# A hybrid decoder layer on one core: substitution rows padded to 36, attention values as one wide product, other stage offsets

## The chip, the cores and the metric

The kernel runs on one core of one Trainium2 chip. Its time is the device time of one execution in microseconds (us); the runs shown are single executions of the same program. The profile is of one further execution and counts its span from the first instruction to the last.

## The reference

One layer of a decoder trunk, 16 meta tokens and 512 frames of width 1024, all in float32. A half-step SwiGLU comes first, then two token mixers that read the same projection, then a second half-step SwiGLU and a norm.

```
h += 1/2 * SwiGLU_1(rmsnorm(h))
P  = rmsnorm(h) @ w_in            # q|k|v, rwkv r|k|v|w|a|g, two gates
A  = sliding-window attention, 16 query heads, 2 key heads, window 128, meta always visible
R  = RWKV-7: per head S = S*w + (S a) b' + v k',  y = S r     (16 heads of 64)
h += (sigmoid(Ga) * (A @ Wa) + sigmoid(Gr) * (R @ Wr)) @ w_out
h += 1/2 * SwiGLU_2(rmsnorm(h))
```

The attention's last steps are `p = e / (sum(e) + exp(sink - m))` and `o = p @ v`. The recurrence S is computed in chunks of 64 tokens; inside a chunk it needs the inverse of a unit lower triangular 64x64 matrix for each head.

## The kernel before

**Stages in time.** In the first 400 us the first SwiGLU runs: weights come by DMA (`raw`), ScalarE makes a rounded copy (`whi`, line 144), VectorE the remainder (`wlo`, line 145), and each product is three matmuls (lines 155 to 157). From 400 to 1130 us the mixer runs, then the output product and the second SwiGLU.

**The mixer** is written as Python generators that `run` interleaves: `qkv`, `attend`, `gates`, `att_branch`, `reload`, `rwkv_branch`, and for each of eight pairs of heads j the stages `stage_a1` (projections, decays), `stage_p` (products of a chunk, the matrices G.g2 to invert), `stage_i` (the inverses), `stage_b` (the recurrence over nine chunks) and `stage_t` (norm, gate). Each task has a start and a span in units of one pair (`PLAN`, plus `SHIFT` for a pair's stage), and `run` always takes the next step of the task whose due time is smallest. `LATE` adds to the priority number under which a step's instructions are handed to the scheduler, so a negative value puts them earlier. The scheduler then fixes one order of instructions for every engine ahead of the run. TensorE (PE), VectorE (DVE), ScalarE (ACT), GpSimd (POOL) and the DMA queue of SyncE (SP) each take their own list strictly in this order, and an instruction that waits holds all behind it on its engine. SP's list holds the loads of weights as well as the stages' own transfers.

**The inverses, `stage_i`.** `stage_p` leaves 32x32 triangles, nine of the upper and eight of the lower half of the chunks for each of the two heads, 34 in all, and writes them to a DRAM tile `Ls` with one triangle in a row. `stage_i` loads `Ls` three times into the tile LT (line 865, `LT<-Ls`), 34 partitions each, 102 in use, and unit columns into X (line 866). Then 31 steps of substitution follow on VectorE, each a product into `xtmp` (line 870) and a sum into X (line 872). The solutions go to the DRAM tile `Xs` (line 876) and from there, transposed, into `xt` (lines 881 and 882). `assemble` completes the 64x64 inverses with two groups of matmuls (lines 898 and 908) that read LT and `xt`. LT and X have one buffer each, so the loads of pair j+1 wait for the end of `assemble` of pair j.

**The recurrence, `stage_b`.** For each chunk: two matmuls with the state W (line 928), a copy `zy` on ScalarE (929), one matmul with `xt` (936), copies into W on VectorE and ScalarE (937, 938), two matmuls (941), and the new state W on VectorE (945 or 947). Each waits for the one before.

**Attention, `attend`.** For each of eight blocks b of 64 queries and two halves i: scores for four groups of 128 rows (x = key head and pair of heads) by at most 208 keys, exponentials `st` in SBUF with their sums `rsum`; `st` transposed by TensorE to `pT` (keys by 512); then, for each of one or two parts of the keys, the product with the values `vt` (line 600: `pT` of one group stands in the array, 64 columns of `vt` move), a multiplication with 1/sum on VectorE (603), a transpose back (608), a copy (611) and two DMAs into `aD` (613).

Of the kernel before, what the change touches and what calls it, by code (L numbers as in the profile page):

```python
# [17 lines left out]
P = 128  # L18
# [18 lines left out]
RB = {"g1": 2, "g2": 2, "W": 2, "g3": 2}  # L37
COUNTS = []
PAUSE = {"sq": 1, "rn": 1, "el": 1, "inv": 1}
PLAN = {"qkv": (-2.771, 0.729), "stage_a1": (-2.83, 0.789), "stage_p": (-1.171, 0.942), "stage_i": (-2.734, 0.587),  # L40
        "stage_b": (-0.138, 0.693), "stage_t": (1.478, 0.214), "att": (-1.614, 1.044), "gate": (0.091, 0.42),
        "att_branch": (3.86, 1.399), "reload": (6.425, 0.417), "rwkv_branch": (7.903, 0.124)}
# [3 lines left out]
SHIFT = {("stage_t", 5): -0.415, ("stage_i", 7): 0.482, ("stage_b", 2): 0.071, ("stage_a1", 6): -0.027, ("stage_i", 4): -0.133,  # L46
        ("stage_t", 2): -0.095, ("stage_b", 3): 0.119, ("stage_p", 1): 0.042, ("stage_t", 4): 0.123, ("stage_t", 3): -0.157,
        ("stage_t", 0): 0.003, ("stage_i", 6): 0.096, ("stage_p", 2): 0.173, ("stage_i", 3): -0.27, ("stage_i", 2): -0.033,
        ("stage_a1", 3): 0.319, ("stage_p", 6): 0.183, ("stage_a1", 4): 0.07, ("stage_p", 3): -0.095, ("stage_i", 1): 0.055,
        ("stage_t", 6): -0.097, ("stage_p", 7): 0.076, ("stage_b", 0): 0.067, ("stage_i", 5): -0.243, ("stage_b", 6): 0.153,  # L50
        ("stage_p", 4): 0.028, ("stage_b", 4): -0.102, ("stage_a1", 0): 0.006, ("stage_a1", 2): 0.186, ("stage_b", 1): -0.009,
        ("stage_t", 7): -0.124, ("stage_t", 1): -0.07, ("stage_i", 0): 0.174, ("stage_p", 5): -0.03, ("stage_b", 7): -0.047}

FIRST = [(0, 0), (0, 1), (1, 0), (1, 1), (27, 0)]
ATTS = 0.946
GATE = 0.462
LATE = {"gate": 337, "att_branch": 1714, "reload": 1055, "rwkv_branch": 2849, "stage_a1": -79, "stage_t": 196, "stage_p": -207,
        "stage_i": -1108, "qkv": -36, "att": 209, "stage_b": 148}
# [50 lines left out]
def hybrid_layer(ctx: ExitStack, tc: tile.TileContext, a, phases="all"):  # L109
# [243 lines left out]
    def mixer(nm):  # L353
# [183 lines left out]
        def attend():  # L537
# [3 lines left out]
            for b in range(NCH):  # L541
# [18 lines left out]
                for i in range(2):  # L560
# [22 lines left out]
                                             accum_out=rsum[:, kv, k:k + 1])  # L583
                    nc.vector.tensor_add(out=rsum, in0=rsum, in1=sm)
                    nc.vector.reciprocal(out=rsum, in_=rsum)
                    yield
                    pTs = []
                    for q, (k0, k1) in enumerate(parts):
# [4 lines left out]
                        nc.scalar.copy(out=pT[:k1 - k0], in_=pt[:k1 - k0])  # L593
                        pTs.append(pT)
                    yield
                    po = bank("att")[:, :4 * CH].rearrange("t (p d) -> t p d", p=4)
                    for x in range(4):
                        kv = x // 2
                        for q, (k0, k1) in enumerate(parts):
                            nc.tensor.matmul(po[:, x, :], pTs[q][:k1 - k0, P * x:P * x + P], vt[:k1 - k0, q, CH * kv:CH * kv + CH],  # L600
                                             start=(q == 0), stop=(q == len(parts) - 1))
                    on = ap.tile([P, 4, CH], F32, name="ao", bufs=1)
                    nc.vector.tensor_tensor(out=on, in0=po, in1=rsum.rearrange("p g k -> p (g k)").unsqueeze(2).to_broadcast([P, 4, CH]),
                                            op=OP.mult)
                    yield
                    pt = bank("att")
                    for kv in range(2):
                        nc.tensor.transpose(out=pt[:, P * kv:P * kv + P], in_=on[:, 2 * kv:2 * kv + 2, :].rearrange("t p d -> t (p d)"),
                                            identity=ident)
                    ao = ap.tile([P, 2, 2, CH], F32, name="ao", bufs=1)  # L610
                    nc.scalar.copy(out=ao, in_=pt[:, :4 * CH].rearrange("p (g x t) -> p g x t", g=2, t=CH))
                    for kv in range(2):
                        nc.sync.dma_start(out=aD[:, 4 * kv + 2 * i:4 * kv + 2 * i + 2, CH * b:CH * b + CH], in_=ao[:, kv])
                    yield

        def gates():
# [151 lines left out]
        def stage_p(j, G):  # L768
# [35 lines left out]
                    m = m.unsqueeze(1).to_broadcast(list(dst.shape))  # L804
                nc.vector.tensor_mul(out=dst, in0=src, in1=m)

            G.Ls = dsc.tile([34, 32, 32], F32, name="Ls")
            for h, U, Vr in ((0, LO, HI), (1, HI, LO)):
                g1, Z, Y = G.g1[h], U, Vr
                pt = bank("s")  # L810
                nc.tensor.matmul(pt[:, 0:P], KBT[:, 0, :], G.g0[:, h, :], start=True, stop=True)
                masked(G.g2[U, 0, :], pt[U, Z], 0)
                masked(G.g0[Vr, h, Z], pt[Vr, Z], 0)
                for c0 in (1, 5):
                    pt = bank("s")
# [12 lines left out]
            nc.tensor.matmul(pb, C("bones"), rkk, start=True, stop=True)
# [27 lines left out]

        def stage_i(j, G):

            Xs = dsc.tile([34, 33, 32], F32, name="Xs")
            G.LT = sp.tile([P, 32, 32], F32, name="LT", bufs=1)  # L860
            LT = G.LT[:102]
            X = sp.tile([102, 11, 32], F32, name="X", bufs=1)
            tmp = sp.tile([102, 11, 32], F32, name="xtmp", bufs=1)
            for q in range(3):
                nc.sync.dma_start(out=LT[34 * q:34 * q + 34], in_=G.Ls)
            nc.sync.dma_start(out=X, in_=a["xinit"])
            yield
            for c in range(31):
                n, w = c // 3 + 1, 31 - c
                nc.vector.tensor_tensor(out=tmp[:, :n, :w], in0=LT[:, c:c + 1, c + 1:32].to_broadcast([102, n, w]),  # L870
                                        in1=X[:, :n, c:c + 1].to_broadcast([102, n, w]), op=OP.mult)
                nc.vector.tensor_add(out=X[:, :n, c + 1:32], in0=X[:, :n, c + 1:32], in1=tmp[:, :n, :w])
                if c % 8 == 7:
                    yield
            for q in range(3):
                nc.sync.dma_start(out=Xs[:, q:33:3, :], in_=X[34 * q:34 * q + 34])
            G.xt = XT[j % 2]
            nc.gpsimd.memset(G.LT[:, :24, :], 0.0)
            for h in range(2):
                u, m = 64 * h, 17 * h  # L880
                nc.sync.dma_start(out=G.xt[u:u + 32, :, u:u + 32], in_=Xs[m:m + 9, 0:32, :].rearrange("c s t -> s c t"))
                nc.sync.dma_start(out=G.xt[u + 32:u + 64, 1:, u + 32:u + 64],
                                  in_=Xs[m + 9:m + 17, 0:32, :].rearrange("c s t -> s c t"))
# [263 lines left out]
def constants():  # L1147
    c = np.zeros((P, NCON), np.float32)

    def put(n, x):  # L1150
        c[:x.shape[0], CON[n]:CON[n] + x.shape[1]] = x
    put("ident", np.eye(P, dtype=np.float32))
    i = np.arange(P)[:, None] % CH
    jj = np.arange(192)[None, :]
    win = np.where((jj > i) & (jj <= 128 + i), 0.0, 8 * NEG).astype(np.float32)
    z = np.zeros((P, NMETA), np.float32)
    put("am", np.concatenate([win, z], 1))
    b = (np.arange(P)[:, None] // CH == np.arange(P)[None, :] // CH).astype(np.float32)
# [16 lines left out]
def prepare(x, meta_tokens, norm_ffn1, ffn1_w_in, ffn1_w_out, norm_mix, w_in, rwkv_mu, sinks, w0, w2, a0, a2, g2, k_k, k_a,  # L1175
# [53 lines left out]
```

## Time and profile before

| what | value |
|---|---|
| three runs | 1551.87, 1556.44 (median), 1558.58 us |
| the profiled execution | 1557.82 us, its span 1556.1 us |
| mean granted TensorE clock | 0.98 |
| TensorE matmul busy, of the span | 1500.3 us (96%) |
| VectorE busy | 900.1 us (58%) |
| ScalarE busy | 652.9 us (42%) |

Busy times are means over stages that differ: VectorE is light in the two SwiGLUs and heavy in the mixer. A matmul's duration in the profile holds the time through the array, in which the next ones already run, so times between starts are shorter than durations. "Idle before" an instruction is the time in which its engine had nothing running, and the name behind it is what ended last before it began.

### The profile page before, as it was taken

The numbers are of one execution on the slowest core, as the hardware profiler recorded it, in microseconds if no ns is written. First come the engines' busy times: TensorE is split into PE (matmuls) and PEld (weight loads), VectorE is DVE, ScalarE is ACT, GpSimd is POOL, SyncE is SP. The second block draws the span as 40 slices with busy tenths as digits, with TensorE's granted clock in tenths as the row PEclk, the third lists the DMA queues.
The fourth block names the chain that finished last, engine by engine and source line by source line (L and its number), as shares of the span: only waits on it lengthen the run. The fifth ranks groups of instructions, "written<-read, shape, count | busy, mean of one in ns | idle before, by whom it ended". The sixth has DMA issues, their size and how long they took to land. (4 is left out here: it accounts for less than half of the span.)

```text
span 1556.1 us, 25641 instructions
## 1 busy us (share of the span) xinstructions
PE 1500.3 (96%) x9365; PEld 1325.2 (85%) x9365; DVE 900.1 (58%) x2471; ACT 652.9 (42%) x1468; POOL 93.6 (6%) x153
## 2 busy tenths in 40 slices
PE   9999999999999999998999999999999999999997
PEld 9999999999887888887878887677777888888886
DVE  6334334344764886887978888675655444443334
ACT  5333333233442457465664754635343333332231
POOL 0111111000100000000000000000000111110000
PEclk9999999999999999999989999999999999999998
DMA  5333333344243333323332232555633333333332
GB/s 165 89 93 91 89 93 88 110 120 116 78 121 96 112 84 89 81 81 104 99 98 76 82 101 85 153 183 173 221 95 89 95 95 96 97 97 91 95 97 79
DMA packets 137838, 163.23 MB, mean 105 GB/s; under 512 B 56960, under 2 KB 68288, under 8 KB 137712
## 3 DMA queue, kind: packets, MB, share of 16 engines
q1 hardware_dynamic: 137568, 161.54, 35.4%
q8 instruction: 73, 1.20, 0.3%
q14 instruction: 53, 0.43, 0.1%
q10 hardware_dynamic: 144, 0.06, 0.0%
HBM read 140.03 MB, written 21.52 MB: 104 GB/s over the span
## 5 line engine op out<-in xcount | busy, mean ns | idle before, releaser
L144 ACT CAST whi<-raw 128x512 fp32r<-128x512 f32 (+1 forms) x426 | 258.8, 611 | 576.6 <-PE dn L156 446.5
L145 DVE TENSOR_TENSOR wlo<-raw,whi 128x512 fp32r<-128x512 f32 (+1 forms) x426 | 287.9, 679 | 304.1 <-ACT whi L144 300.0
L155 PE MATMUL dn<-uh,whi 128*128 128x264 f32 (+1 forms) x1320 | 426.8, 323 | 1.9 <-DVE tgt L657 0.9
L156 PE MATMUL dn<-ul,whi 128*128 128x264 f32 (+1 forms) x1320 | 427.3, 324 | 0.3 <-DVE ul L203 0.3
L157 PE MATMUL dn<-uh,wlo 128*128 128x264 f32 (+1 forms) x1320 | 425.0, 322 | 0.0
L155 PEld LDWEIGHTS dn<-uh,whi 128*128 128x128 f32 x1320 | 247.8, 188 | 23.9 <-ACT whi L144 3.2
L157 PEld LDWEIGHTS dn<-uh,wlo 128*128 128x128 f32 x1320 | 248.4, 188 | 19.9
L156 PEld LDWEIGHTS dn<-ul,whi 128*128 128x128 f32 x1320 | 248.4, 188 | 19.0 <-DVE ul L203 0.5
L155 PE MATMUL pdn<-uh,whi 128*128 128x264 f32 (+3 forms) x656 | 229.0, 350 | 4.6 <-ACT whi L144 2.5
L157 PE MATMUL pdn<-uh,wlo 128*128 128x264 f32 (+3 forms) x656 | 224.3, 343 | 3.7 <-DVE wlo L145 3.6
L156 PE MATMUL pdn<-ul,whi 128*128 128x264 f32 (+3 forms) x656 | 224.5, 343 | 0.9 <-DVE ul L253 0.8
L155 PEld LDWEIGHTS pdn<-uh,whi 128*128 128x128 f32 x656 | 127.1, 194 | 17.0 <-ACT whi L144 4.2
L157 PEld LDWEIGHTS pdn<-uh,wlo 128*128 128x128 f32 x656 | 127.0, 194 | 11.4 <-DVE wlo L145 5.0
L156 PEld LDWEIGHTS pdn<-ul,whi 128*128 128x128 f32 x656 | 126.7, 193 | 7.7 <-DVE ul L253 1.7
L155 PE MATMUL dn<-mh,whi 128*128 128x264 f32 (+2 forms) x350 | 110.7, 316 | 0.0
L156 PE MATMUL dn<-ml,whi 128*128 128x264 f32 (+2 forms) x350 | 110.6, 316 | 0.0
L157 PE MATMUL dn<-mh,wlo 128*128 128x264 f32 (+2 forms) x350 | 110.5, 316 | 0.0
L285 POOL TENSOR_TENSOR sg<-sg,rstd 128x528 f32<-128x528 f32 (+1 forms) x44 | 58.0, 1319 | 595.8 <-ACT sg L284 428.9
L286 DVE TENSOR_TENSOR m<-sg,dn 128x528 f32<-128x528 f32 (+1 forms) x44 | 30.6, 696 | 70.9 <-PE dn L157 67.6
L155 PEld LDWEIGHTS dn<-mh,whi 128*128 128x128 f32 x350 | 66.1, 189 | 4.4
L156 PEld LDWEIGHTS dn<-ml,whi 128*128 128x128 f32 x350 | 66.1, 189 | 4.3
L157 PEld LDWEIGHTS dn<-mh,wlo 128*128 128x128 f32 x350 | 66.0, 189 | 4.3
(395 smaller groups left out, 2058.2 us busy)
## 6 DMA issues: line engine op xcount, KB each, us to landing
raw<-win SPq DMA_DIRECT2D x104, 256.0 KB
raw<-w1in SPq DMA_DIRECT2D x88, 256.0 KB
raw<-w2in SPq DMA_DIRECT2D x88, 256.0 KB
raw<-w1out SPq DMA_DIRECT2D x40, 256.0 KB
raw<-w2out SPq DMA_DIRECT2D x40, 256.0 KB
gD<-tgt SPq DMA_DIRECT2D x24, 256.0 KB
raw<-wa SPq DMA_DIRECT2D x16, 256.0 KB
tgt<-gD SPq DMA_DIRECT2D x16, 256.0 KB
```

Source lines behind the costliest of these rows:

```text
L144: nc.scalar.copy(out=hi, in_=raw)
L145: (eng or nc.vector).tensor_tensor(out=lo, in0=raw, in1=hi.bitcast(F32), op=OP.subtract)
L155: nc.tensor.matmul(o, hi, xh[k][:, c], start=(k == 0), stop=False)
L156: nc.tensor.matmul(o, hi, xl[k][:, c], start=False, stop=False)
L157: nc.tensor.matmul(o, lo, xh[k][:, c], start=False, stop=last)
L285: nc.gpsimd.tensor_mul(out=sg, in0=sg, in1=nm.rstd[:, :n])
L286: nc.vector.tensor_mul(out=vw(m), in0=vw(sg), in1=vu)
```

## The change

Three things change. The rows of `Ls`, `Xs`, LT, X and `xtmp` become 36 (18 for each head) and 108 instead of 34 and 102: the lower half has a ninth row for the meta chunk, which is written and solved but not read back. The attention multiplies `st` by 1/sum before it is transposed, and takes the product with the values as one matmul for each part of the keys: `vt` (both key heads, 128 columns) stands in the array and all 512 columns of `pT` move. Its result lies with the value channels on partitions, so the transpose back falls away; of each key head's 64 rows only the 256 columns of its own queries are copied out, by two copies, and one DMA writes `aD`. The rows of the packed attention weights (`wa`) are put in the matching order on the host. Third, the tables `PLAN`, `SHIFT` and `LATE` and the spacing `ATTS` get other numbers.

```diff
-PLAN = {..., "stage_i": (-2.734, 0.587), ...
+PLAN = {..., "stage_i": (-1.378, 0.919), ...
...
-LATE = {..., "stage_i": -1108, "qkv": -36, "att": 209, "stage_b": 148}
+LATE = {..., "stage_i": -1815, "qkv": -42, "att": 209, "stage_b": 148}
 # attend
                     nc.vector.reciprocal(out=rsum, in_=rsum)
+                    sv = st.rearrange("p g k s -> p (g k) s")[:, :, :n]
+                    nc.vector.tensor_tensor(out=sv, in0=sv, in1=rsum.rearrange("p g k -> p (g k)").unsqueeze(2).to_broadcast([P, 4, n]),
+                                            op=OP.mult)
                     yield
...
-                    po = bank("att")[:, :4 * CH].rearrange("t (p d) -> t p d", p=4)
-                    for x in range(4):
-                        kv = x // 2
-                        for q, (k0, k1) in enumerate(parts):
-                            nc.tensor.matmul(po[:, x, :], pTs[q][:k1 - k0, P * x:P * x + P], vt[:k1 - k0, q, CH * kv:CH * kv + CH], ...)
-                    on = ap.tile([P, 4, CH], F32, name="ao", bufs=1)
-                    nc.vector.tensor_tensor(out=on, in0=po, in1=rsum...to_broadcast([P, 4, CH]), op=OP.mult)
+                    po = bank("att")
+                    for q, (k0, k1) in enumerate(parts):
+                        nc.tensor.matmul(po, vt[:k1 - k0, q, :], pTs[q][:k1 - k0], start=(q == 0), stop=(q == len(parts) - 1))
                     yield
-                    pt = bank("att")
-                    for kv in range(2):
-                        nc.tensor.transpose(out=pt[:, P * kv:P * kv + P], in_=on[:, 2 * kv:2 * kv + 2, :]..., identity=ident)
-                    ao = ap.tile([P, 2, 2, CH], F32, name="ao", bufs=1)
-                    nc.scalar.copy(out=ao, in_=pt[:, :4 * CH].rearrange("p (g x t) -> p g x t", g=2, t=CH))
-                    for kv in range(2):
-                        nc.sync.dma_start(out=aD[:, 4 * kv + 2 * i:4 * kv + 2 * i + 2, CH * b:CH * b + CH], in_=ao[:, kv])
+                    ao = ap.tile([P, 4, CH], F32, name="ao", bufs=1)
+                    pv = po.rearrange("p (g x t) -> p g x t", g=2, t=CH)
+                    for kv, rows in enumerate((LO, HI)):
+                        nc.scalar.copy(out=ao[rows], in_=pv[rows, kv])
+                    nc.sync.dma_start(out=aD[:, 4 * i:4 * i + 4, CH * b:CH * b + CH], in_=ao)
 # stage_p
-            G.Ls = dsc.tile([34, 32, 32], F32, name="Ls")
+            G.Ls = dsc.tile([36, 32, 32], F32, name="Ls")
...
-                nc.sync.dma_start(out=G.Ls[17 * h + 9:17 * h + 17]..., in_=G.g2[u + 32:u + 64, 1:, 32:64])
+                nc.sync.dma_start(out=G.Ls[18 * h + 9:18 * h + 18]..., in_=G.g2[u + 32:u + 64, :, 32:64])
 # stage_i
-                nc.sync.dma_start(out=LT[34 * q:34 * q + 34], in_=G.Ls)
+                nc.sync.dma_start(out=LT[36 * q:36 * q + 36], in_=G.Ls)
...
-                nc.sync.dma_start(out=Xs[:, q:33:3, :], in_=X[34 * q:34 * q + 34])
+                nc.sync.dma_start(out=Xs[:, q:33:3, :], in_=X[36 * q:36 * q + 36])
```

**Where instructions move.** On VectorE, at the start of the substitution of pair 4 (`xtmp<-LT,X` is its first step, `kbt` are `stage_p`'s products for a later pair, `W` the state of the recurrence that runs at that time). Before:

```order
L937 COPY W<-pn 64x64
L870 TENSOR_TENSOR xtmp<-LT,X 102x31
L584 TENSOR_TENSOR rsum<-rsum,sm 128x4
L792 SCALAR_TENSOR_TENSOR kbt<-tal,tE_9024 64x8x64
L872 TENSOR_TENSOR X<-X,xtmp 102x31
L585 RECIPROCAL rsum<-rsum 128x4
L794 SCALAR_TENSOR_TENSOR kbt<-tal,tE_9024 64x16
L870 TENSOR_TENSOR xtmp<-LT,X 102x30
L792 SCALAR_TENSOR_TENSOR kbt<-tk,tE_9024 64x8x64
L872 TENSOR_TENSOR X<-X,xtmp 102x30
L947 SCALAR_TENSOR_TENSOR W<-py,f,sf 64x64
```

The same place after the change (`st<-st,rsum` is the new multiplication, `wlo<-raw,whi` the remainder of a weight block):

```order
L787 SCALAR_TENSOR_TENSOR kbt<-tal,tE_8959 64x8x64
L789 SCALAR_TENSOR_TENSOR kbt<-tal,tE_8959 64x16
L787 SCALAR_TENSOR_TENSOR kbt<-tk,tE_8959 64x8x64
L584 TENSOR_TENSOR rsum<-rsum,sm 128x4
L789 SCALAR_TENSOR_TENSOR kbt<-tk,tE_8959 64x16
L585 RECIPROCAL rsum<-rsum 128x4
L587 TENSOR_TENSOR st<-st,rsum 128x832
L446 SCALAR_TENSOR_TENSOR tk<-pdn,omm,tm 128x264
L933 COPY W<-pn 64x64
L145 TENSOR_TENSOR wlo<-raw,whi 128x512 x2
L941 TENSOR_SCALAR W<-py,f 64x64 x2
L866 TENSOR_TENSOR xtmp<-LT,X 108x31
```

Before, the products `kbt` and the next state W stood behind the first step of the substitution; now they stand ahead of it.

On SP, from the store of the solutions to the loads of `xt`, for pair 4. Before:

```order
L986 DMA g2w<-g2s 128x256
L624 DMA gD<-tgt 128x512
L876 DMA Xs<-X 374x1x32 x3
L881 DMA xt_4608<-Xs 32x9x32
L882 DMA xt_4608<-Xs 32x8x32
```

And after the change:

```order
L994 DMA rD<-tys 128x512
L872 DMA Xs<-X 396x1x32 x3
L608 DMA aD<-ao 128x4x64
L143 DMA raw<-win 128x512 x2
L877 DMA xt_4608<-Xs 32x9x32
L878 DMA xt_4608<-Xs 32x8x32
```

Two loads of weights and one store of attention now stand between the store of the solutions and the loads of `xt`.

On TensorE, block 1 of the attention (`patt<-con,st` are transposes of `st`, `patt<-vt,pT` the product with the values, `pdn` a projection, `ps` products of `stage_p`). Before:

```order
L591 MATMUL patt<-con,st 16x128 x4
L837 MATMUL ps<-con,kbt 128x128 x4
L157 MATMUL pdn<-uh,wlo 128x512
L600 MATMUL patt<-vt,pT 128x64 x8
L837 MATMUL ps<-con,kbt 128x128 x4
L845 MATMUL ps<-con,tv 16x128
L155 MATMUL pdn<-uh,whi 128x512
L156 MATMUL pdn<-ul,whi 128x512
L608 MATMUL patt<-con,ao 128x128 x2
```

After:

```order
L594 MATMUL patt<-con,st 16x128 x4
L156 MATMUL pdn<-ul,whi 128x512
L157 MATMUL pdn<-uh,wlo 128x512
L155 MATMUL pdn<-uh,whi 128x512
L156 MATMUL pdn<-ul,whi 128x512
L602 MATMUL patt<-pT,vt 128x512 x2
L157 MATMUL pdn<-uh,wlo 128x512
```

Eight narrow products and two transposes have become two wide products.

More of the change, by code (lines that the diff above doesn't have):

```diff
@@ L39 @@
 PAUSE = {"sq": 1, "rn": 1, "el": 1, "inv": 1}
-PLAN = {"qkv": (-2.771, 0.729), "stage_a1": (-2.83, 0.789), "stage_p": (-1.171, 0.942), "stage_i": (-2.734, 0.587),
-        "stage_b": (-0.138, 0.693), "stage_t": (1.478, 0.214), "att": (-1.614, 1.044), "gate": (0.091, 0.42),
-        "att_branch": (3.86, 1.399), "reload": (6.425, 0.417), "rwkv_branch": (7.903, 0.124)}
+PLAN = {"qkv": (-2.725, 0.766), "stage_a1": (-2.739, 0.789), "stage_p": (-1.216, 0.962), "stage_i": (-1.378, 0.919),
+        "stage_b": (0.017, 0.693), "stage_t": (1.509, 0.192), "att": (-1.581, 1.044), "gate": (0.017, 0.425),
+        "att_branch": (3.926, 0.992), "reload": (6.358, 0.258), "rwkv_branch": (7.491, 0.149)}
@@ L43 @@
 STEPS = {"qkv": 30, "stage_a1": 19, "stage_p": 13, "stage_i": 9, "stage_b": 27, "stage_t": 5, "att": 13, "gate": 2, "att_branch": 24, "reload": 7,
          "rwkv_branch": 16}
-SHIFT = {("stage_t", 5): -0.415, ("stage_i", 7): 0.482, ("stage_b", 2): 0.071, ("stage_a1", 6): -0.027, ("stage_i", 4): -0.133,
-        ("stage_t", 2): -0.095, ("stage_b", 3): 0.119, ("stage_p", 1): 0.042, ("stage_t", 4): 0.123, ("stage_t", 3): -0.157,
-        ("stage_t", 0): 0.003, ("stage_i", 6): 0.096, ("stage_p", 2): 0.173, ("stage_i", 3): -0.27, ("stage_i", 2): -0.033,
+SHIFT = {("stage_t", 5): -0.415, ("stage_i", 7): 0.36, ("stage_b", 2): 0.071, ("stage_a1", 6): -0.027, ("stage_i", 4): -0.613,
+        ("stage_t", 2): -0.095, ("stage_b", 3): 0.119, ("stage_p", 1): 0.042, ("stage_t", 4): 0.159, ("stage_t", 3): -0.157,
+        ("stage_t", 0): 0.003, ("stage_i", 6): 0.096, ("stage_p", 2): 0.173, ("stage_i", 3): -0.295, ("stage_i", 2): -0.235,
@@ L54 @@
 FIRST = [(0, 0), (0, 1), (1, 0), (1, 1), (27, 0)]
-ATTS = 0.946
+ATTS = 0.961
 GATE = 0.462
-LATE = {"gate": 337, "att_branch": 1714, "reload": 1055, "rwkv_branch": 2849, "stage_a1": -79, "stage_t": 196, "stage_p": -207,
-        "stage_i": -1108, "qkv": -36, "att": 209, "stage_b": 148}
+LATE = {"gate": 160, "att_branch": 1153, "reload": -297, "rwkv_branch": 3776, "stage_a1": -79, "stage_t": 196, "stage_p": -207,
+        "stage_i": -1815, "qkv": -42, "att": 209, "stage_b": 148}
 S_DECAY = float(np.exp(np.float32(-0.5)))
@@ L823, in stage_p @@
                 u = 64 * h
-                nc.sync.dma_start(out=G.Ls[17 * h:17 * h + 9].rearrange("c s t -> s c t"), in_=G.g2[u:u + 32, :, 0:32])
-                nc.sync.dma_start(out=G.Ls[17 * h + 9:17 * h + 17].rearrange("c s t -> s c t"), in_=G.g2[u + 32:u + 64, 1:, 32:64])
+                nc.sync.dma_start(out=G.Ls[18 * h:18 * h + 9].rearrange("c s t -> s c t"), in_=G.g2[u:u + 32, :, 0:32])
+                nc.sync.dma_start(out=G.Ls[18 * h + 9:18 * h + 18].rearrange("c s t -> s c t"), in_=G.g2[u + 32:u + 64, :, 32:64])
             yield
@@ L857, in stage_i @@
         def stage_i(j, G):
-            Xs = dsc.tile([34, 33, 32], F32, name="Xs")
+            Xs = dsc.tile([36, 33, 32], F32, name="Xs")
             G.LT = sp.tile([P, 32, 32], F32, name="LT", bufs=1)
-            LT = G.LT[:102]
-            X = sp.tile([102, 11, 32], F32, name="X", bufs=1)
-            tmp = sp.tile([102, 11, 32], F32, name="xtmp", bufs=1)
+            LT = G.LT[:108]
+            X = sp.tile([108, 11, 32], F32, name="X", bufs=1)
+            tmp = sp.tile([108, 11, 32], F32, name="xtmp", bufs=1)
             for q in range(3):
-                nc.sync.dma_start(out=LT[34 * q:34 * q + 34], in_=G.Ls)
+                nc.sync.dma_start(out=LT[36 * q:36 * q + 36], in_=G.Ls)
             nc.sync.dma_start(out=X, in_=a["xinit"])
@@ L869, in stage_i @@
                 n, w = c // 3 + 1, 31 - c
-                nc.vector.tensor_tensor(out=tmp[:, :n, :w], in0=LT[:, c:c + 1, c + 1:32].to_broadcast([102, n, w]),
-                                        in1=X[:, :n, c:c + 1].to_broadcast([102, n, w]), op=OP.mult)
+                nc.vector.tensor_tensor(out=tmp[:, :n, :w], in0=LT[:, c:c + 1, c + 1:32].to_broadcast([108, n, w]),
+                                        in1=X[:, :n, c:c + 1].to_broadcast([108, n, w]), op=OP.mult)
                 nc.vector.tensor_add(out=X[:, :n, c + 1:32], in0=X[:, :n, c + 1:32], in1=tmp[:, :n, :w])
@@ L879, in stage_i @@
             for h in range(2):
-                u, m = 64 * h, 17 * h
+                u, m = 64 * h, 18 * h
                 nc.sync.dma_start(out=G.xt[u:u + 32, :, u:u + 32], in_=Xs[m:m + 9, 0:32, :].rearrange("c s t -> s c t"))
                 nc.sync.dma_start(out=G.xt[u + 32:u + 64, 1:, u + 32:u + 64],
-                                  in_=Xs[m + 9:m + 17, 0:32, :].rearrange("c s t -> s c t"))
+                                  in_=Xs[m + 10:m + 18, 0:32, :].rearrange("c s t -> s c t"))
             yield
@@ L1159, in constants @@
     put("bones", b)
-    x = np.zeros((102, 11, 32), np.float32)
+    x = np.zeros((108, 11, 32), np.float32)
     for gcol in range(3):
@@ L1163, in constants @@
             if 3 * ii + gcol < 32:
-                x[34 * gcol:34 * gcol + 34, ii, 3 * ii + gcol] = 1
+                x[36 * gcol:36 * gcol + 36, ii, 3 * ii + gcol] = 1
     return c, x
```

12 lines of the change are left out of this document (3 added, 9 removed).

## The prediction

> **What bounds the kernel now.** I read the page's head first, then the busy times by stage, then who waits in the mixer, and last the seconds around those waits. The runs' 0.5% (7.8 us of the median) is about what a measurement of this kernel can tell from no change.
>
> ```profile
> span 1556.1 us, 25641 instructions
> PE 1500.3 (96%) x9365; PEld 1325.2 (85%) x9365; DVE 900.1 (58%) x2471; ACT 652.9 (42%) x1468; POOL 93.6 (6%) x153
> ```
> ```profile
> core 0: us, PE busy (x) PEld busy (x) DVE busy (x) ACT busy (x) POOL busy (x), PEclk, DMA share, GB/s
> 0.00:400.00 400.00, 397.51 (x3222) 395.17 (x3222) 168.72 (x263) 137.65 (x224) 30.24 (x31) 1.00 0.36 106
> 530.00:1060.00 530.00, 497.35 (x3159) 425.67 (x3157) 416.91 (x1601) 296.61 (x855) 24.36 (x69) 0.96 0.36 104
> 1130.00:1556.00 426.00, 415.16 (x1882) 341.85 (x1880) 180.68 (x308) 134.74 (x219) 28.59 (x22) 0.99 0.32 93
> ```
>
> TensorE bounds the whole, and in the two SwiGLUs (first and last row) it hardly idles at full clock. The change touches only the mixer. There, from 530 to 1060 us, TensorE idles 530 - 497.4 = 32.6 us and its granted clock is 0.96, so some 21 us more of clock are missing. VectorE is busy 417 of 530 us (79%). So what the change can save is work on TensorE, idle time, and half-clock time of this stretch. Who waits there:
>
> ```profile
> L870 DVE TENSOR_TENSOR xtmp<-LT,X x248: 163/220/259, 544.0 to 1037.9; 102x84 f32<-102x84 f32 x12, 102x54 f32<-102x54 f32 x8, 102x90 f32<-102x90 f32 x8, 102x72 f32<-102x72 f32 x8
> ...
>   DMA LT<-Ls: 10.8, 5
>   issue: 3.2, 1
>   DMA vt<-vD: 2.7, 1
> ```
> ```profile
> 796.83 0.19 DVE L870 TENSOR_TENSOR xtmp<-LT,X 102x31 f32<-102x31 f32 x1 [3.17 <-issue]
> ...
> 799.00 0.65 PE L928 MATMUL pn<-W,g1e 128*128 128x64 f32 x2 [2.74 <-DVE W L947]
> ...
> 866.52 0.19 DVE L870 TENSOR_TENSOR xtmp<-LT,X 102x31 f32<-102x31 f32 x1 [2.77 <-DMA LT<-Ls]
> ...
> 868.40 0.69 PE L928 MATMUL pn<-W,g1e 128*128 128x64 f32 x2 [2.07 <-DVE W L947]
> ...
> 938.79 0.19 DVE L870 TENSOR_TENSOR xtmp<-LT,X 102x31 f32<-102x31 f32 x1 [2.62 <-DMA LT<-Ls]
> ...
> 940.91 0.67 PE L941 MATMUL py<-W,g 128*128 128x64 f32 x4 [2.23 <-DVE W L937]
> ```
>
> The first step of the substitution stops VectorE seven times, 10.8 + 3.2 + 2.7 = 16.7 us, in seven of the eight pairs, whatever name the row gives the releaser. Behind it in VectorE's list stands the state W, so TensorE stops each time: in the three pairs shown 2.74 + 2.07 + 2.23 = 7.04 us for 3.17 + 2.77 + 2.62 = 8.56 us, or 0.82 us for each. The transfer is slow:
>
> ```profile
> 927.38 1.01 SPq L865 DMA_DIRECT2D LT<-Ls  x3
> ...
> 1039.20 4.70 SPq L876 DMA_DIRECT2D Xs<-X  x3
> ...
> 1048.04 0.33 SPq L881 DMA_DIRECT2D xt<-Xs  x1
> ...
> 1049.41 0.46 SPq L882 DMA_DIRECT2D xt<-Xs  x1
> ```
> ```profile
> 1050.96 0.46 PE L936 MATMUL pn<-zy,xt 128*128 128x128 f32 x2 [2.79 <-DMA xt<-Xs]
> ```
> ```profile
>   DMA xt<-Xs: 7.9, 5
> ```
>
> LT (three loads of 136 KB) is issued at 927.4 and VectorE goes on at 938.8, 11.4 us later. The store of the solutions is issued at 1039.2, and the reads of it start only at 1048.0, 8.8 us later. The last read, of 32 KB with 32 rows outermost, releases TensorE 1.55 us after its start. All loads of `xt` together cost TensorE 7.9 us in five waits (the last row, from line 936). And after a stop the clock is halved:
>
> ```profile
> 546.50:553.30 6.80, 6.80 (x32) 6.71 (x33) 5.30 (x30) 3.81 (x14) 0.06 (x1) 0.50 0.12 39
> 799.10:809.30 10.20, 10.20 (x43) 9.61 (x44) 5.45 (x21) 4.82 (x13) 0.00 (x0) 0.50 0.19 61
> 867.40:874.20 6.80, 5.79 (x18) 4.77 (x18) 5.31 (x23) 3.12 (x8) 0.00 (x0) 0.50 0.12 31
> 942.40:945.80 3.40, 3.40 (x13) 2.80 (x13) 2.85 (x16) 2.69 (x10) 0.00 (x0) 0.51 0.04 15
> 1051.70:1058.50 6.80, 6.12 (x22) 5.51 (x23) 2.02 (x6) 2.74 (x9) 0.00 (x0) 0.50 0.56 190
> ```
>
> Four windows follow a stop at LT, the fifth the stop at `xt`; the granted clock there is 0.50. TensorE's busy time in them, 26.2 and 6.1 us, would take half at full clock: 13.1 and 3.1 us are lost.
>
> **The change, part by part.**
>
> Attention's products on TensorE.
>
> ```profile
> 553.35 1.00 PE L600 MATMUL patt<-vt,pT 80*128 80x64 f32 x8
> ...
> 555.56 0.38 PE L608 MATMUL patt<-con,ao 128*128 128x128 f32 x2
> ```
> ```profile
> L600 PE MATMUL patt<-vt,pT x240: 217/275/421, 553.3 to 982.1; 80*128 80x64 f32 x56, 128*128 128x64 f32 x56, 16*128 16x64 f32 x8
> ...
> L608 PE MATMUL patt<-con,ao x32: 270/273/421, 555.6 to 983.6; 128*128 128x128 f32 x32
> ```
> ```profile
> L828 PE MATMUL ps<-tsx,con x16: 591/592/667, 531.5 to 974.3; 128*128 128x512 f32 x16
> ```
> ```profile
> 779.13 1.02 PE L828 MATMUL ps<-tsx,con 128*128 128x512 f32 x2
> ```
>
> Removed: 240 passes (two for each float32 product) at 1.00/8 = 0.125 us, 30.0 us, and 32 transposes at 0.38 - 0.273 = 0.11 us, 3.5 us. Added: 30 products, 60 passes of 512 columns; the nearest row is line 828, two passes of that shape in 1.02 us of which the last takes 0.592, so 0.43 us from start to start: 25.7 us. Net -7.8 us. If the narrow passes between other work cost only 0.112 (0.9 of the row), it is -4.7. I take -7.
>
> LT. With 36 rows instead of 34 the transfer's new time is not in this trace. Its bounds are no change (11.4 us from issue to use) and the 1.55 us of the `xt` load. I take some 3 us, near the fast end, since the bytes do not explain 11.4: at the stretch's mean of 104 GB/s, with all its other loads in it, 408 KB take 3.9 us. [...] All of it gone is 0.82 x 16.7 = 13.7 us. VectorE's new order helps as well, since `kbt` and W now stand ahead of the first step. I take -12; between 0 and -13.7.
>
> `xt`. The store loses its slow issue (4.70 us for three) and the wait after it. SP then waits less for its own store, and the weight loads queued behind come earlier. But for some pairs weight loads now stand between. I take -5.5 of 7.9; between 0 and -7.9.
>
> Clock. Of 16.2 us I take -9.5, in the proportion of the stops that go, less what other stops bring; between 0 and -16.2. [...]
>
> VectorE and ScalarE.
>
> ```profile
> L603 DVE TENSOR_TENSOR ao<-patt,rsum 128x256 f32<-128x256 f32 x16 | 6.7, 416 | 8.7 <-PE patt L600 8.5
> ...
> L829 DVE TENSOR_TENSOR tsx<-tv,ps 128x512 f32<-128x512 f32 x8 | 5.4, 678 | 0.0
> ```
> ```profile
> L611 ACT COPY ao<-patt 128x256 f32<-128x256 f32 x16 | 5.9, 371 | 7.2 <-PE patt L608 6.2 <-DVE ny L335 0.7 <-DVE gy L335 0.2
> ...
> L854 ACT COPY W<-ps 64x256 f32<-64x256 f32 x16 | 5.8, 366 | 0.2
> ```
>
> From 256 to 512 columns a product grows by 0.262 us, so 832 columns take 0.678 + 320 x 0.262/256 = 1.0 us, 576 take 0.74 and 320 take 0.48: 12 + 2 + 2 of them are 14.4 us, less the 6.7 of line 603: VectorE gets +7.7 us. It stands in line ahead of W copies, and VectorE is busy 79% of the time, so about half reaches TensorE: +4; between 0 (it fills VectorE's waits) and +7.7. The transposes of `st` now wait for it, which takes the place of TensorE's wait for line 603. ScalarE has two copies of 0.366 for one of 0.371 us, 16 times: +5.8 us on an engine busy 297 of 530 us (56%): +1; between 0 and +5.8. The 6 added partitions cost the substitution nothing, since its steps are as long in elements per partition as before. SP's 16 fewer stores I cost at nothing, and the rewritten tables too: the covers between the recurrence's steps are alike in both orders.
>
> Sum: -7 - 12 - 5.5 - 9.5 + 4 + 1 = -29 us. The profiled execution took 1557.8, which is 1.4 above the median; 1557.8 - 29 = 1528.8.
>
> **The rivals.**
>
> The clock stays. Half-clock windows come from other stops as well, and nothing is won there: 1557.8 - 29 + 9.5 = 1538. [...]
>
> The padding does nothing. The slowness of LT has another cause (its reads following on the writes of `Ls`, or a full queue). Then LT, `xt` and the clock stay, and -7 + 4 + 1 leaves 1556, no change. For it: the trace shows no transfer with 36 rows. Against it: the load of `xt` goes through the same DRAM in 1.55 us.
>
> SP's list holds `xt` and LT back (slower). The three moved weight loads and others can be issued only when a `raw` buffer is free:
>
> ```profile
> SPq L143 <- DVE wlo L145: 768.6, 335, 18.8
> ```
>
> That is 2.3 us for each such wait, 18.8 at most. Where two stand ahead of `xt` or LT, 4.6 us go. A microsecond of lateness costs TensorE 0.82 and, at 13.1 of clock for 13.7 of stops, 0.78 more. It decides from the point where the transfers come later than now, that is over 8 us of holding back for LT. At 3 us later than now in seven pairs it adds 7 x 3 x 1.6 = 34 us to the 1556 of the rival before: 1590. Against it: only pairs 3 and 4 have weight loads between.
>
> **How the numbers follow.** My forecast, waits and most of the clock gone, 0.67; the clock stays 0.13; padding without effect 0.11; SP holding back 0.09. All bounds at their good end give 1557.8 - 7.8 - 13.7 - 7.9 - 16.2 = 1512. At the other end the forecast with half of its three waiting terms gives 1542, and the rival without effect 1556; a part of that rival has to be in the range, so 1511 to 1553. Faster by over 0.5% (below 1548.7) are the forecast and the clock rival, 0.80; within 0.5%, 0.11; slower, 0.09.
>
> **What would show it.** Right: `xtmp` no longer waits for LT; the reads of `xt` are issued some 4 us after the store; the idle time of 32.6 us in the recurrence falls below 20 and the granted clock there rises to 0.98; line 602 takes about 1.0 us for each product. Wrong: waits for `xt` or LT stay above 10 us, or TensorE waits for the 832-wide product, or the clock stays at 0.96 with the waits gone.

## The result and the profile after

The changed kernel takes 1530.63 us (median of five runs, 1528.48 to 1534.80), against 1554.2 us for the kernel before in the runs beside it: a ratio of 0.985, 95% interval 0.9825 to 0.9874. So it is 1.5% faster. The profiled execution took 1530.27 us, close to the forecast of 1529.

The head of the changed kernel's page, and its mixer row of the busy times by stage (same columns as before):

```profile
span 1528.5 us, 25204 instructions
PE 1483.8 (97%) x9153; PEld 1291.9 (85%) x9153; DVE 909.4 (59%) x2471; ACT 659.1 (43%) x1484; POOL 94.1 (6%) x153
```
```profile
530.00:1060.00 530.00, 505.88 (x3081) 411.56 (x3079) 444.13 (x1656) 320.52 (x916) 24.42 (x67) 0.99 0.39 114
```

TensorE's idle time over the span fell from 1556.1 - 1500.3 = 55.8 to 44.7 us. In 530 to 1060 us it is 24.1 instead of 32.6 us, and the granted clock there is 0.99 instead of 0.96. VectorE is busier, 444 for 417 us.

Who waits at the substitution's first step (the line's own view, its idle time and what ended it), and at the products with `xt` (line 932, formerly 936):

```profile
L866 DVE TENSOR_TENSOR xtmp<-LT,X x248: 161/224/259, 537.4 to 1006.2; 108x84 f32<-108x84 f32 x12, 108x54 f32<-108x54 f32 x8, 108x90 f32<-108x90 f32 x8, 108x72 f32<-108x72 f32 x8
...
  DVE ss L722: 0.2, 1
```
```profile
  ACT zy L925: 16.7, 49
```

The 16.7 us in seven pairs are down to 0.2, and no load of LT is named. At the products the 7.9 us for `xt` are gone; they now wait for `zy`, 16.7 us in 49 small pieces (11.3 before). On SP's list the store of the solutions and the first reads of them, for the first pair, read (start, duration):

```profile
577.25 2.58 SPq L872 DMA_DIRECT2D Xs<-X  x3
579.93 0.48 SPq L544 DMA_DIRECT2D qb<-qD  x1
580.46 1.13 SPq L547 DMA_DIRECT2D kx<-kD  x2
581.76 0.46 SPq L877 DMA_DIRECT2D xt<-Xs  x1
```

From the store's issue to the first read are 4.5 us here and 4.1 to 6.0 in the eight pairs, where 8.4 to 9.0 were. The three stores hold SP's queue 2.58 us. The mixer has five stretches at half clock where the trace of before has ten, 51.2 us long in all (busy times of the five stretches; the column after POOL is the granted clock):

```profile
471.30:474.70 3.40, 3.40 (x9) 2.64 (x8) 0.73 (x2) 0.00 (x0) 0.00 (x0) 0.51 0.53 125
512.20:515.60 3.40, 3.40 (x16) 3.35 (x16) 3.34 (x11) 1.41 (x3) 0.00 (x0) 0.50 0.00 0
539.50:542.90 3.40, 3.40 (x16) 3.40 (x17) 3.34 (x14) 1.70 (x6) 0.00 (x0) 0.50 0.21 74
631.70:635.10 3.40, 3.40 (x14) 2.71 (x14) 3.21 (x19) 1.34 (x2) 0.31 (x2) 0.50 0.27 88
979.80:983.20 3.40, 3.40 (x12) 2.80 (x12) 2.55 (x9) 1.36 (x4) 0.00 (x0) 0.51 0.80 262
```

Each is 3.4 us long, 17 us in all; before, stretches of 6.8 and 10.2 us stood at the stops. The attention's new instructions, from the groups by line (busy, mean ns, then idle time before them):

```profile
L602 PE MATMUL patt<-pT,vt 80*128 80x512 f32 (+2 forms) x60 | 31.2, 610 | 0.0
L594 PE MATMUL patt<-con,st 128*80 128x128 f32 (+2 forms) x120 | 20.4, 275 | 2.5 <-ACT pT L596 1.6 <-DVE st L587 0.9
...
L587 DVE TENSOR_TENSOR st<-st,rsum 128x832 f32<-128x832 f32 (+2 forms) x16 | 14.7, 919 | 0.1
...
L607 ACT COPY ao<-patt 64x256 f32<-64x256 f32 x32 | 11.7, 366 | 9.2 <-PE patt L602 9.0
```

A product with the values takes 31.2/30 = 1.04 us, the normalisation 14.7 us in all, and TensorE waits for it 0.9 us. Nearly all of this is as forecast, and by it alone the prediction looks right. The experiments show that not all of its terms are.

### The profile page after: what moved, and what is told of

It reads as the page before. It is cut to its first block, busy times and chain, and to the rows that moved or that the text cites. A ratio compares the mean times of both kernels' runs of the same rounds, so it can differ in the third digit from the quotient of the medians.

```text
span 1528.5 us, 25204 instructions
## 1 busy us (share of the span) xinstructions
PE 1483.8 (97%) x9153; PEld 1291.9 (85%) x9153; DVE 909.4 (59%) x2471; ACT 659.1 (43%) x1484; POOL 94.1 (6%) x153
## 5 line engine op out<-in xcount | busy, mean ns | idle before, releaser
L156 PE MATMUL pdn<-ul,whi 128*128 128x264 f32 (+3 forms) x656 | 221.0, 338 | 1.8 <-DVE ul L253 1.8
L156 PEld LDWEIGHTS pdn<-ul,whi 128*128 128x128 f32 x656 | 126.2, 193 | 10.2 <-DVE ul L253 2.6
L157 PEld LDWEIGHTS pdn<-uh,wlo 128*128 128x128 f32 x656 | 125.5, 192 | 10.8 <-DVE wlo L145 2.9
```

What stands on the lines that cost most here:

```text
L156: nc.tensor.matmul(o, hi, xl[k][:, c], start=False, stop=False)
L157: nc.tensor.matmul(o, lo, xh[k][:, c], start=False, stop=last)
```

## The experiments

**Theories.** The prediction's: padding takes the stops away (27 us with the clock), attention nets 2 us (7 off TensorE, 4 and 1 back), the offsets bring nothing of their own. The rival: the new order and offsets carry the gain, and the padding could not have done it in the old order. All times are medians; each ratio is against the kernel before, run beside it (1555 to 1556 us).

| kernel | rows | attention | offsets | us | ratio (95%) |
|---|---|---|---|---|---|
| fixed buffers only (b34) | 34 | old | old | 1555.7 | 1.0005 (0.9987 to 1.0023) |
| padding, order of before (b36) | 36 | old | old | 1519.6 | 0.977 (0.975 to 0.9789) |
| LT padded, `Xs` not (lt36) | 36/34 | old | old | 1530.4 | 0.985 (0.9829 to 0.987) |
| the change, fixed buffers (a36) | 36 | new | new | 1530.1 | 0.9836 (0.9821 to 0.9851) |
| the change with 38 rows (a38) | 38 | new | new | 1591.9 | 1.0238 (1.0214 to 1.0261) |
| attention alone (k_att) | 34 | new | old | 1561.4 | 1.0046 (1.0028 to 1.0063) |
| offsets alone (k_off) | 34 | old | new | 1574.1 | 1.0123 (1.0098 to 1.0147) |
| padding as written (k_pad) | 36 | old | old | 1523.7 | 0.9802 (0.9781 to 0.9824) |
| padding and attention (k_padatt) | 36 | new | old | 1524.6 | 0.9802 (0.9786 to 0.9818) |
| padding and offsets (k_padoff) | 36 | old | new | 1521.7 | 0.9781 (0.976 to 0.9802) |
| as k_padatt, no normalisation (nonorm) | 36 | new | old | 1522.2 | 0.9794 (0.9777 to 0.9811) |
| as k_padatt, diagonal (diag) | 36 | new | old | 1538.2 | 0.9892 (0.9877 to 0.9906) |

**The padding in the unchanged order.** Any part of the change makes the scheduler order the rest anew. To keep the order, only the rows of the tiles are changed and `Ls` comes from two fixed DRAM buffers, so that its padding is always filled. Every engine's list then stays as it was, but for two short transfers on SP ahead of the recurrence (the texts of the expectations say four).

```diff
+        LS = [dram.tile([36, 32, 32], F32, name=f"Ls{i}") for i in range(2)]   # filled once
...
-            G.Ls = dsc.tile([34, 32, 32], F32, name="Ls")
+            G.Ls = LS[j % 2]
-            Xs = dsc.tile([34, 33, 32], F32, name="Xs")
+            Xs = dsc.tile([36, 33, 32], F32, name="Xs")
...
-                nc.sync.dma_start(out=LT[34 * q:34 * q + 34], in_=G.Ls)
+                nc.sync.dma_start(out=LT[36 * q:36 * q + 36], in_=G.Ls)
...
-                nc.sync.dma_start(out=Xs[:, q:33:3, :], in_=X[34 * q:34 * q + 34])
+                nc.sync.dma_start(out=Xs[:, q:33:3, :], in_=X[36 * q:36 * q + 36])
```

Expected: 

> The kernel before with the padding alone: LT, X, Xs and Ls get 36 rows for 34 and every engine's instructions stand in the order of before, so that only the transfers' shape differs (Ls is taken from two fixed buffers that four short transfers at the start fill; rows 34 and 35 are padding). Theory of the prediction: the padded transfers fan out and the stops at them go, so LT's wait of 16.7 us at xtmp falls below 3 us, xt's of 7.9 us at u's products below 2 us, the granted clock in 530 to 1060 us rises from 0.96 to 0.98, and the time falls by 12 + 5.5 + up to 9.5 us from 1555, to 1528 to 1540 us. Rival 1, the gain comes from the new order and offsets (the stops lie where other work could not fill them in either case): 1550 to 1557 us. Rival 2, the rows are no faster with 36 than with 34: 1555 us, with both waits as before.

Measured: 1519.64 us (1514.78 to 1521.33), 36 us faster than before, 11 us faster than the whole change, and below all three ranges of the expectation. Its page, its mixer row by stage, and its granted clock beside that of before and of the changed kernel:

```profile
span 1513.1 us, 25645 instructions
PE 1478.7 (98%) x9365; PEld 1308.2 (86%) x9365; DVE 901.1 (60%) x2471; ACT 652.2 (43%) x1468; POOL 93.0 (6%) x153
```
```profile
530.00:1060.00 530.00, 518.80 (x3381) 442.00 (x3381) 443.19 (x1673) 318.36 (x909) 24.36 (x69) 1.00 0.40 119
```
```profile
core 0: 1556.1 us, clock 0.980
```
```profile
core 0: 1513.1 us, clock 0.994
```
```profile
core 0: 1528.5 us, clock 0.991
```

Idle time fell from 55.8 to 34.4 us (-21.4). The same 9365 matmuls are busy 1478.7 instead of 1500.3 us (-21.6), and the clock accounts for that: 0.020 of 1556.1 is 31.1 us not granted, 0.006 of 1513.1 is 9.1, a difference of 22.0. These two executions are 43 us apart, however, where the medians are 36: the clock of 0.980 lies below that of all fifteen executions of the kernel before beside this run (0.982 to 0.988), and 0.994 is the highest of this kernel's five (0.990 to 0.994). On average over these executions 23.6 and 13.7 us were not granted. By that some 10 of the 36 us are clock and some 26 are waits, an estimate that counts time at half clock as half lost. No wait for LT or `xt` is left in any list. The rival falls: the padding needs no new order.

The control has the fixed buffers with 34 rows. Expected: 

> The kernel before with Ls in two fixed buffers of 34 rows, filled by the same four short transfers at the start, and no other row moved: the control for the padding in the order of before. If the fixed buffers do nothing: 1552 to 1559 us with the waits for LT and xt of before. If they carry part of the 36 us: below 1545 us.

Measured: 1555.7 us, no difference. The first step of the substitution waits 17.0 us there, 9.5 of it under the name of LT<-Ls. So the 36 us are the rows'.

**LT's share and xt's.** X is stored from 34 of each 36 rows, so that LT's loads are padded and the stores are not:

```diff
-                nc.sync.dma_start(out=Xs[:, q:33:3, :], in_=X[36 * q:36 * q + 36])
+                nc.sync.dma_start(out=Xs[:, q:33:3, :], in_=X[36 * q:36 * q + 34])
```

Expected: 

> As the run with the padding alone in the order of before (1519.6 us), but Xs has 34 rows again: X is stored from its first 34 rows of each group of 36, so LT's loads keep the 36-row form and the stores that feed xt get the 34-row form back; no engine's order moves. By the prediction's terms LT carries 12 and xt 5.5 us, and the clock's share goes with the stops: the waits for xt<-Xs come back at 8 to 16 us over 10 to 12 places, and the time is 1526 to 1535 us. Rival: xt carries the gain and LT's stops cost little, since VectorE is not the bound: 1545 to 1555 us. Other rival: all of it is LT's, 1518 to 1522 us.

Measured: 1530.42 us, inside the range that the prediction's terms gave. LT's loads bring 25 us, the stores another 11. The clock of these five executions, 0.989 to 0.993, is that of the full padding, so the whole gain in clock came with LT's loads (some 10 of their 25 us), and the 11 us of the stores are waits. The waits that came back, from the list of waits (engine and line waited for, us, times, longest):

```profile
DVE LT L897 <- DMA xt<-Xs: 8.4, 6, 1.9
...
PE pn L939 <- DMA xt<-Xs: 3.0, 4, 1.4
...
PEld pn L939 <- DMA xt<-Xs: 2.4, 2, 1.8
```

VectorE's wait of 8.4 us, at a transpose of `xt`, has its like in the trace of before (8.2 us), and the prediction did not count it: it took only TensorE's 7.9 us (5.4 here).

**The transfers in the new order.** The changed kernel with 38 rows, and with 36 rows in the same fixed buffers; the order of the engines is that of the change.

```diff
-            Xs = dsc.tile([36, 33, 32], F32, name="Xs")
+            Xs = dsc.tile([38, 33, 32], F32, name="Xs")
...
-                nc.sync.dma_start(out=LT[36 * q:36 * q + 36], in_=G.Ls)
+                nc.sync.dma_start(out=LT[38 * q:38 * q + 38], in_=G.Ls)
```

Expected with 38 rows: 

> The changed kernel with 38 rows for 36 in LT, X, Xs and Ls, in the same order of instructions on every engine (Ls from two fixed buffers, as in the run beside it; the offset of the second head stays 18). [...] If the transfers' shape carries the gain: LT is again late at xtmp by some 2 to 3 us in each of 8 pairs (11.4 us from issue to use against the 8.4 to 9 us that the new order leaves), xt by 1 to 4 us, and the time is 1540 to 1556 us. If the new order and offsets carry it, since they leave LT more time: 1530 to 1535 us and no wait for LT over 3 us in sum.

Expected with 36 rows: 

> The changed kernel with Ls from two fixed buffers of 36 rows that four short transfers at the start fill, and nothing else moved: what the fixed buffers, which the runs with 36 and 38 rows also have, do by themselves. If they do nothing: 1527 to 1535 us, like the changed kernel (1530.6). If they carry part of the gain in the order of before: 10 us or more faster, near 1518.

Measured: 1591.92 and 1530.09 us. The fixed buffers do nothing in this order either, and two more rows cost 62 us. The page's head, the waits and the store with 38 rows:

```profile
span 1588.8 us, 25209 instructions
PE 1499.2 (94%) x9153; PEld 1307.4 (82%) x9153; DVE 911.3 (57%) x2471; ACT 659.8 (42%) x1484; POOL 93.2 (6%) x153
```
```profile
PEld py L940 <- DVE W L936: 23.5, 20, 5.3
DVE LT L893 <- DMA xt<-Xs: 18.9, 9, 4.2
...
DVE xtmp L869 <- DMA LT<-Ls: 15.7, 5, 4.9
DVE xtmp L869 <- issue: 9.4, 2, 6.0
...
DVE xtmp L869 <- DMA g2w<-g2s: 3.9, 1, 3.9
```
```profile
584.84 5.20 SPq L875 DMA_DIRECT2D Xs<-X  x3
```

The first step of the substitution waits in all eight pairs, 15.7 + 9.4 + 3.9 = 29.0 us, and the store holds SP's queue 5.20 us for 2.58. Idle time is 89.6 us for 44.7, and with a granted clock of 0.977 some 36.5 us of clock are missing for 13.8. From the issue of LT's loads to the first step are 13.4 and 11.2 us with 38 rows (the first two pairs) and 10.5 to 12.0 with the 34 of before, and only 7.7 to 9.6, without a wait, in the changed kernel. So of the three it is the 36 rows that come early, not more rows or more bytes. The traces show these times, not their cause, nor whether padded transfers fan out, as the theory in the expectation of the padding has it. The expectation's 1540 to 1556 us was far too low: it took for 38 rows the 11.4 us of 34, which no run had shown, and reckoned 2 to 3 us in each pair, where 3.6 came, and left out what TensorE then waits for W (23.5 us) and the clock.

**The parts alone, with 34 rows.** The attention's lines as in the change's diff, or its four tables of offsets, in the kernel before.

Expected of the attention: 

> The attention part alone (one product of 512 columns per pair of rows of keys, the 832-wide normalisation on VectorE, the rows of the branch's weight packed to match), with before's 34 rows and before's offsets; the scheduler puts the rest in a new order round it. Prediction's term: 7 us less on TensorE (4.7 to 7.8), 4 us more on VectorE, 1 us on ScalarE, so 1549 to 1553 us with the stops at LT (16.7 us) and xt (7.9 us) left. Rival 1: TensorE's saving is not on the path, 1554 to 1557 us. Rival 2: the new order that comes with it moves more than the products do, and the time lies 10 us or more off 1551 on either side.

Expected of the offsets: 

> The stage offsets alone (PLAN, SHIFT, ATTS and LATE of the changed kernel), with before's 34 rows and before's attention products. Prediction: offsets cost or bring nothing of their own beside the waits; with 34 rows stage_i starts later against what needs it, so LT's wait stays above 10 us: 1552 to 1562 us. Rival: the offsets themselves take the stops at LT away by giving the loads more time, 1535 to 1545 us, with LT's wait below 5 us.

Measured: 1561.38 and 1574.05 us. Both are slower, the attention by 5.6 us and the offsets by 18. The first lies 10.4 us off 1551, where the expectation's second rival (the new order) begins, the second above both of its ranges. With the attention alone VectorE waits for LT, and TensorE for the 832-wide product, at the weight loads and the matmuls of the same transposes (list of waits):

```profile
DVE xtmp L865 <- DMA LT<-Ls: 16.1, 6, 3.8
...
PEld patt L594 <- DVE st L587: 3.9, 2, 3.0
...
PE patt L594 <- DVE st L587: 3.3, 2, 2.6
```

With the offsets alone the wait for LT stays (13.3 us) and more is lost at `xt` (10.8 us on VectorE). They did not give the loads time. Some 11 of their 18 us are clock (0.974 to 0.982 in its six executions); what the rest is was not worked out.

**The parts together with 36 rows.** The same edits on top of the padding as the change writes it (second head at row 18).

Expected of the padding as written: 

> The padding as the change writes it (36 rows, the second head at row 18, its loads of 9 rows), with the attention products and the offsets of before; the scheduler orders some thousand rows anew for it. The instructions are those of the run with the padding in the order of before (1519.6 us), so the distance between the two is what a new order by itself can do. If the order is worth little: 1516 to 1523 us, and then the attention products cost the change 5 us (1524.6 with them) and its offsets 2 us (1521.7). If a new order alone moves some us: 1524 us or more, or 1512 or less, and then neither of those is larger than the order's own scatter.

Expected with the attention: 

> Padding and attention products of the change with the offsets of before (PLAN, SHIFT, ATTS, LATE). Set against the padding alone in the order of before (1519.6 us): if the attention part brings its 7 us less on TensorE, 1511 to 1516 us; if, as the attention part alone had it (1561.4 against 1555.8), it costs some 5 us through VectorE or the order that comes with it, 1522 to 1528 us. If the changed kernel's offsets are needed with it: 1531 us or more.

Expected with the offsets: 

> Padding and offsets of the change with the attention products of before. If the new offsets cost something of their own even with 36 rows (alone with 34 rows they cost 18 us): 1527 to 1540 us. If they only cost where LT and xt are late: 1517 to 1523 us. If the attention products bring 7 us to the whole change, this run lies 7 us above it, at 1537 to 1538 us.

Measured: 1523.72, 1524.60 and 1521.66 us; with both, which is the change, 1530.63. The padding as written lies 4.1 us above the padding in the old order, with intervals that just overlap, so the new order and the ninth row are worth a few us at most. On top of it the attention moves the time by +0.9 and the offsets by -2.1, neither of which is told from nothing, and both together by +6.9 (+6.4 with the fixed buffers). That is little more than the 4.1 us which the new order of the padding may have cost. What became of TensorE's saving, from the page's head and the groups by line without and with the new attention:

```profile
PE 1479.3 (97%) x9365; PEld 1304.6 (86%) x9365; DVE 899.0 (59%) x2471; ACT 652.9 (43%) x1468; POOL 93.5 (6%) x153
...
L600 PE MATMUL patt<-vt,pT 128*128 128x64 f32 (+1 forms) x240 | 33.5, 276 | 0.6 <-ACT pT L593 0.5
...
L608 PE MATMUL patt<-con,ao 128*128 128x128 f32 x32 | 6.5, 276 | 0.2 <-DVE ao L603 0.2
```
```profile
PE 1478.2 (97%) x9153; PEld 1288.2 (85%) x9153; DVE 907.2 (60%) x2471; ACT 660.4 (43%) x1484; POOL 93.7 (6%) x153
...
L602 PE MATMUL patt<-pT,vt 80*128 80x512 f32 (+2 forms) x60 | 31.0, 612 | 0.3 <-ACT pT L596 0.3
```

The rows of the passes fall from 33.5 + 6.5 = 40.0 to 31.0 us, 9.0 in all, though they overlap with others. TensorE as a whole is busy only 1.1 us less; the granted clock of these two executions is 0.996 and 0.993, 4.6 us of the span, and without that it would be 5.7 less, an estimate. With spans of 1518.6 and 1522.5 us its idle time rises from 39.3 to 44.3. So the work saved turned into idle time. Of the clock little is certain: over all their executions the two kernels have 0.992 to 0.996 and 0.991 to 0.995.

**Is it the product on VectorE?** Once it is left out, so that the attention values are not divided by their row sums, and once it is replaced by four diagonal matrices in the transposes, which stand in a buffer of `pT`:

```diff
-                    nc.vector.tensor_tensor(out=sv, in0=sv, in1=rsum...to_broadcast([P, 4, n]), op=OP.mult)
+                    dg = ap.tile([P, 512], F32, name="pT").rearrange("p (x t) -> p x t", x=4)      # second kernel only
+                    nc.vector.tensor_tensor(out=dg, in0=ident...to_broadcast([P, 4, P]), in1=rsum...to_broadcast([P, 4, P]), op=OP.mult)
...
-                            nc.tensor.transpose(out=pt[...], in_=st[:, x // 2, x % 2, k0:k1], identity=ident)
+                            nc.tensor.matmul(pt[...], st[:, x // 2, x % 2, k0:k1], dg[:, x, :], start=True, stop=True)
```

Expected without it: 

> Padding and attention products of the change with the offsets of before (1524.6 us), with the 832-wide product on VectorE left out: the attention values are not divided by their row sums. 16 products of 1.02 us fall away and the order is made anew. Theory: this product ahead of the transposes holds VectorE's queue and takes the attention products' gain: 1511 to 1518 us, below the padding alone. Rival: the products cost nothing on the path and the loss against 1519.6 us is the order's: 1522 to 1528 us.

Expected with the diagonal: 

> As the run with padding, attention products of the change and offsets of before (1524.6 us), but the row sums go into the transposes: each transpose becomes a product with a diagonal matrix that holds one over the row sums, and VectorE fills four such matrices with one product of 512 columns in place of the 832-wide one. VectorE then saves about 0.4 us in each of 16 places (1.02 us for 832 columns, in proportion 0.63 for 512). If VectorE's product is what takes the gain: 1514 to 1522 us. If not: 1522 to 1528 us, or more where the products with the diagonal take TensorE longer than the transposes did.

Measured: 1522.23 and 1538.15 us. Without the product VectorE is busy 898.2 instead of 907.2 us, and the time is 2.4 us shorter, with overlapping intervals: the product does not hide a gain of 7 us. With the diagonal the group of transposes becomes

```profile
L594 PE MATMUL patt<-pT,st 128*80 128x128 f32 (+2 forms) x240 | 36.4, 280 | 1.2 <-DVE pT L587 1.1
...
L587 DVE TENSOR_TENSOR pT<-con,rsum 128x512 f32<-128x512 f32 x16 | 10.9, 679 | 0.0
```

so 240 passes for 120, 36.4 for 20.6 us; VectorE's product saves 3.7. The time rises by 13.6 us: TensorE is busy 14.1 us more and idles 1.4 us less at the same clock (0.993). Work added here costs nearly its full price, and work removed brought nothing. One reason would be that the removed passes lay beside waits of the recurrence while the added ones lengthen attention's own row of steps (`st`, `pT`, product, copy); no run shows that. Nor is it settled why attention and offsets together cost 6.9 us, when neither does alone. The two differ from the padding by a new order of over a thousand rows, of which only the sum was measured.

## Why the prediction was right, and where its steps were wrong

The forecast was 29 us of gain and 23.6 came, in 1530.6 us for 1529. That the time came so near is in part luck. The forecast counted down from a profiled execution of 1557.8 us, 3.6 above the median beside the changed kernel. And the sum hides two errors of opposite sign: in the order of before the padding gives 36 us where the terms said 27, and the rest of the change takes 11 back where the terms said 2 more of gain (4.1 with the padding as written, 6.9 with attention and offsets together).

- **LT and xt (-12 and -5.5), with the clock (-9.5).** That the padding takes the stops away was right. Together they measured -36.2, of which some 10 are clock by all executions and some 26 waits. So the clock was forecast well (the 22 us between the two profiled executions are an accident of which ones were profiled), though five stretches next to the named stops were taken for it where the mixer has ten. The term that was mis-sized is `xt`: 11 us for 5.5, above its bound of 7.9. VectorE's wait of 8.2 us for it was left out, which would be about the difference; that it all lay on the path is not shown. LT brought 25 us, some 15 without the clock, for the 12 forecast.
- **Attention on TensorE (-7).** The passes were priced well (9.0 us less by their rows, some 5.7 by TensorE's busy time at equal clock, 4.7 to 7.8 forecast), the step from work to time failed. The term held that TensorE's work in the mixer is time. The head of the page says 96% busy, but in this stretch the recurrence, attention and VectorE release one another, and what TensorE saved it idled. Measured in time, each with the new order that came with it: +0.9 with 36 rows and the old offsets, +5.6 with 34 rows, +9.0 with 36 rows and the new offsets.
- **VectorE and ScalarE (+4, +1).** The wide product measured 14.7 us in all as forecast (14.4), and the 6 added partitions were free: the 248 products of the substitution take 54.1 us for 53.7, its sums 53.7 for 53.6. The run without it is 2.4 us faster, which is not told from nothing, so the +4 is neither shown nor excluded. TensorE's matmuls wait for it 0.9 us in the changed kernel, 3.3 where LT is late as well. ScalarE's +1 was not measured by itself.
- **The tables at nothing.** Wrong with 34 rows (+18), right with 36 and the old attention (-2.1), +6.0 with the new one.
- **Transfer times.** The reads of `xt` start 4.1 to 6.0 us after the store, as said (some 4). The changed kernel starts the substitution 7.7 to 9.6 us after the loads of LT, without waiting, so the transfer's own time is not seen, only that it is less than that. The 3 us taken for it were the author's estimate between two bounds, and no run shows them.
- **The marks.** The idle time from 530 to 1060 us did not fall below 20 (24.1); in the padding alone it does (11.2). The clock came out at 0.99 for the 0.98 said, in the execution that was profiled.
- **The rivals.** "The padding does nothing" and "the clock stays" are excluded by the padding in the old order. "SP's list holds them back" did not happen with 36 rows. Its price of 1.6 us for each microsecond of lateness is not confirmed: 36.2 us for the 24.6 us of stops that it counts are 1.5 each, but with VectorE's 8.2 us at `xt`, which went too, 1.1.

The best version is the padding alone in the order of before, 1519.6 us: 2.3% faster than the kernel before, 0.7% faster than the change.

## What to carry to other kernels

Price a stop on the engine that bounds the kernel at its length plus the half-clock time that the trace shows at it (some 10 of 36 us here), and take the clock from all executions: one profile of each kernel gave 22 us for it. Look on every engine for who waits for a late transfer, since VectorE's wait was the one left out. Look for a transfer's slowness in its number of rows before its bytes: two rows of padding were worth 36 us here, and two more cost the changed kernel 62. And take each part of a change by itself with the order of the rest held still, since a sum that comes out right may be two errors.

## What the runs showed of the hardware that was not expected

The granted clock was 0.50 or 0.51 for 3.4 us at a time in the changed kernel, and the stops ahead of two such stretches were shorter than that. TensorE was busy 2.58 of the 4.5 us ahead of the stretch at 539.5, with one long stop (first row):

```profile
539.50 0.75 PE L807 MATMUL ps<-g,kbt 128*128 128x128 f32 x2 [1.92 <-ACT st L582]
```
```profile
978.97 0.50 PE L156 MATMUL pdn<-ul,whi 128*128 128x512 f32 x1 [0.59 <-DVE ul L253]
```

Ahead of the stretch at 979.8 TensorE was busy 2.80 of 3.8 us, and no stop was longer than the 0.59 us of the second row. The stretches at half clock that are shown here and in the prediction last 3.4, 6.8 or 10.2 us. Not every stop has one: in the kernel before TensorE stopped for 2.58 us up to 735.35, and the granted clock was 1.00 in the stop and in the 9.65 us behind it.

```profile
735.35 0.44 PE L608 MATMUL patt<-con,ao 128*128 128x128 f32 x2 [2.58 <-DVE ao L603]
```
```profile
735.35:745.00 9.65, 9.65 (x54) 7.40 (x55) 8.79 (x42) 9.27 (x23) 0.10 (x1) 1.00 0.50 155
```

What decides it is not shown.

How long SP's queue is held by an issue also changes with the number of rows. Three stores of X hold it 4.2 to 4.7 us with 34 rows (the kernel before), 2.4 to 2.6 with 36 (the changed kernel) and 4.7 to 5.2 with 38 (its first five pairs). The three loads of LT go the other way, 0.9 to 1.0, 1.1 to 1.2 and 0.9 us. Why is not shown.
